# Weight and token rows that run on over group borders, with the input norm and the head issued in another order

## The chip, the cores and the metric

The kernel runs on one core of a Trainium2 chip. A core has five engines with a queue each: TensorE (PE in the profile, with its weight loads as PEld), VectorE (DVE), ScalarE (ACT), GpSimd (POOL) and SyncE (SP), which here only starts transfers. Transfers from the device's memory are started on the queues of SP, ACT and POOL. The metric is the device time of one execution in microseconds; lower is better.

## The reference

One step of a decoder layer for 256 prompt tokens and 8 sample tokens, all in float32, model width 2048. All weight products of the layer run over the 264 tokens together.

```python
def layer(x, conv_buf, h0, C0, n0, m0, mk, mv, ...):
    xn = rmsnorm(x, g_mix)
    z = xn @ w_in                                  # 2048 -> 5128
    xr, conv_new = causal_conv(z[..., OFF_RGX:OFF_RGG], conv_buf, conv_w, conv_b)
    r = jax.nn.sigmoid(block_diag(xr, w_rg_a, b_rg_a))
    ig = jax.nn.sigmoid(block_diag(xr, w_rg_x, b_rg_x))
    h_rg, h_last = rglru(xr, r, ig, rg_lambda, h0)  # uses softplus(-rg_lambda)
    y_rg = rmsnorm((h_rg * jax.nn.gelu(z[..., OFF_RGG:OFF_Q])), g_rg_out)
    ...
    h_ml, C_new, n_new, m_new = mlstm(q, k, v, logi, logf, C0, n0, m0)
    h_ml = rmsnorm(h_ml, g_ml_out.reshape(ML_HEADS, ML_DV)).reshape(B, L, ML_WIDTH)
    y_ml = h_ml * jax.nn.sigmoid(z[..., OFF_O:OFF_I])
    x = x + jnp.concatenate([y_rg, y_ml], axis=-1) @ w_out
    xq = (rmsnorm(x, g_xa) @ w_xa_q).reshape(B, L, XA_HEADS, XA_DH)
    ...                                            # attention over 256 memory tokens
    x = x + o @ w_xa_o
    xf = rmsnorm(x, g_ffn)
    x = x + (jax.nn.silu(xf @ w_ffn_gate) * (xf @ w_ffn_up)) @ w_ffn_down   # 2048 -> 5632 -> 2048
```

The memory's keys and values (`mem @ w_xa_k`, `mem @ w_xa_v`, after a norm) and a last norm of x come on top; the states and the keys and values are outputs too.

## The kernel before

**Tiles.** Activations stand transposed: 128 features on the partitions, 264 tokens along them. A feature chunk c of 128 is one row of 264 words, and four chunks share a tile of the pool `B` (26 tiles of `SLOT` = 1088 words); the norms' and products' operands are `HL` pairs, one tile for the high and one for the low part. A weight block (2048 inputs by 128 outputs) comes in two halves into `raw` (5 tiles) by SP's queue. `split_half` writes its high part on ACT (a copy rounded to fp32r) and its low part on DVE (the difference) into a tile `W` (4 tiles): per chunk a row of 264 words, 128 high, 128 low and 8 unused. So each row, of weights and of tokens, starts 1,056 bytes behind the one before it, which is 32 bytes more than four times 256. A half has 8 rows in two groups of four; the second group starts `SLOT` words behind the first, 32 words (128 bytes) further than the rows would have run on. The tile of the next four token chunks starts at a slot of its own in the same way. Both borders fall together, after every fourth chunk.

**Steps.** The list `steps` holds one step for each weight block. A step runs 16 chunks, each with the three matmuls of `mm3` (weights high with tokens high, high with low, low with high; the weights are the stationary operand, 264 token columns stream), so 48 matmuls into one of four PSUM banks `mm`. `evac` functions read the bank one step later. Steps 0 to 3 are special (`pe_first`): each takes four chunks of the tokens for all four first outputs, so that work can begin before all of x is there; their four banks (two `ax`, two `mm`) are read out after step 3. Then come the rest of `w_in`, `w_out`, the attention's q, k, v, o and, from about half of the time on, the feed-forward blocks.

**Side work.** Recurrences, gates, norms and attention are Python generators (`rg_gen`, `ml_gates`, `ml_norm`, `mem_gen` and others) that `pump` advances between the issue of two steps, by priced clocks of DVE and ACT. Small products in them write banks `ax`: `token_sums` sums a row of squares over the partitions (one output column for each 128 tokens, in plain fp32, which the profile shows as two matmuls each), and `spread` lays the resulting column out along the tokens again.

**Order.** Only SP's order is that of the code. On the other engines a scheduler orders the instructions by a simulated time line and by priorities, so the place in the code isn't the place on the engine.

**Head.** x (`xres`) and the first weights come on SP's queue in the order x 0-1, weights, x 2-3, weights and so on; the small vectors `vecs` on ACT's queue in two pieces. `warm(7)` runs seven matmuls on ones before there is data. The input norm adds up squares of 16 chunks with 16 ACT operations and 15 DVE additions into `acc_x` during steps 1 to 4 (`sumsq`); its token sums, the reciprocal root on DVE (`rsqrt`, tiles `c`) and the spread are `norm_x`, issued after step 4; ACT then writes `rstd`, which the evacuations of the first outputs need. `rg_coef` (with `log1p`) makes a coefficient out of `rg_lambda` by 20 small DVE operations on tiles `t` of 8 columns, and one on ACT.

In the profile most instructions carry line 63, that of the helper `Engine`; tiles tell them apart.

Of the kernel before, what the change touches and what calls it, by code (L numbers as in the profile page):

```python
# [10 lines left out]
F32 = mybir.dt.float32  # L11
# [6 lines left out]
P = 128  # L18
# [6 lines left out]
H = 4  # L25
# [58 lines left out]
def layer_kernel(ctx: ExitStack, tc, xT, memT, vec, wrg, w_in, w_out, w_q, w_k, w_v, w_o,  # L84
# [26 lines left out]
    def B(shape, dt=F32, skip=0):  # L111
        return view(sb.tile([P, SLOT], dt, tag="B", bufs=NB, name=nm("B")), shape, skip)
# [8 lines left out]
    class Arr:  # L121


        def __init__(self, nb, w=N, dt=F32):
            self.t, self.nb, self.w, self.dt = {}, nb, w, dt

        def tile(self, q):
            if q not in self.t:
                self.t[q] = B([P, min(4, self.nb), self.w], self.dt)
            return self.t[q]  # L130

        def __call__(self, c):
# [1 line left out]

    class HL:
        def __init__(self, nb, w=N):
            self.h, self.l = Arr(nb, w, F32R), Arr(nb, w, F32R)

        def __call__(self, c):
            return self.h(c), self.l(c)  # L140
# [1 line left out]
    class Side:  # L142
# [5 lines left out]
        def both(self, c):  # L148
            q, j = divmod(c, 2)
            if q not in self.t:  # L150
                self.t[q] = B([P, 2, 2 * T + 8], F32R, skip=16 * (q % 2))
            return self.t[q][:, j, : 2 * T]

        def __call__(self, c):
# [28 lines left out]
    def split_half(i, h, parts=1):  # L183
        if i >= len(steps):
            return
        cols = steps[i][1]
        lo, hi = h * 1024, min(cols, (h + 1) * 1024)
        w = sb.tile([P, 2, SLOT], F32R, tag="W", bufs=4, name=nm("W"))
        ng = (hi - lo) // 512
        rows = w[:, 0:ng, LEAD: LEAD + 4 * ROW].rearrange("p g (r x) -> p g r x", x=ROW)  # L190
        raw = raws[i, h][:, : hi - lo].rearrange("p (g r x) -> p g r x", r=4, x=P)
        pieces = [(slice(0, ng), slice(0, 4))]
        if parts > 1:
            pieces = [(slice(g, g + 1), slice(r, r + 8 // parts)) for g in range(ng) for r in range(0, 4, 8 // parts)]
        fused = i == GATES
        with tc.high_priority():
            for g, r in pieces:
                src, wh = raw[:, g, r, :], rows[:, g, r, 0:P]
                low = rows[:, g, r, P: 2 * P]
                if fused:  # L200
                    wh, low, src = wh[:, :, :, 0:64], wh[:, :, :, 64:P], src[:, :, :, 0:64]
                st["split"] = act.activation(wh, src, AF.Copy)
                dve.tensor_sub(low, src, wh)
        splits[i, h] = w

    class W:
# [1 line left out]
            self.i = i  # L208

        def __call__(self, c):  # L210
            w, g, o = splits[self.i, c // 8], c % 8 // 4, LEAD + c % 4 * ROW
            return w[:, g, o: o + P], w[:, g, o + P: o + 2 * P]

        def wide(self, c):
            w = splits[self.i, c // 2][:, c % 2, LEAD: LEAD + 4 * ROW].rearrange("p (r x) -> p r x", x=ROW)
            return w[:, :, 0:P], w[:, :, P: 2 * P]

    def mm3(ps, a, b, start, stop):
# [42 lines left out]
    def finish(cond):  # L261

        for _ in range(10000):
            if cond():
                return
            pump(1e12)
        raise RuntimeError("side work does not end")

    def bank(tag="mm"):
        return psm.tile([P, 512], F32, tag=tag, bufs=4, name=nm(tag))  # L270
# [294 lines left out]
    def ml_gates():  # L565
        R = ml["R"]
        li, u, e, lf, b, g, M = (R(j)[0:4] for j in range(7))
        yield STEP
        dve.scalar_tensor_tensor(e, u, -1.0, u, op0=OP.mult, op1=OP.min)
        act.activation(e, e, AF.Exp)  # L570
        yield 0.4
        log1p(lf, e)
        yield 6.0
        dve.tensor_scalar(u, u, 0.0, None, op0=OP.min)
        dve.tensor_sub(lf, u, lf)

# [24 lines left out]
        i4 = ident[0:4, 0:4]  # L601
        for j in range(2):
            pe.transpose(ps[:, 64 + 4 * j: 68 + 4 * j], g[:, j * P: j * P + P], i4)
        for j, w0 in enumerate(WIN):
            pe.transpose(ps[:, 72 + 4 * j: 76 + 4 * j], b[:, w0: w0 + P], i4)
# [185 lines left out]
    def ml_norm():  # L791

        while not (ml["pg"].done and ml["sg"].done):
            yield STEP
        hh = hT["t"]
        a = B([P, H, N])
        for h in range(H):
            for vb in range(2):
                act.activation(hh(2 * h + vb)[:, T:N], nums[:, 2 * h + vb, :], AF.Copy)
            sumsq(a[:, h, :], hh(2 * h), True)  # L800
            sumsq(a[:, h, :], hh(2 * h + 1), False)
            yield 0.35
        yield STEP
        ps = bank("ax")
        for h in range(H):
# [460 lines left out]
    with tc.high_priority():  # L1266
        for c in range(KC):
            split(*xn(c), xres[:, c, :], V("g_mix", c))
            if c == 1:
                split_half(0, 0, 4)  # L1270
            elif c == 3:
                split_half(0, 1, 2)

    pend = []
    for i, (src, cols, pef, evf, need) in enumerate(steps):
# [145 lines left out]
```

## Time and profile before

| | us |
|---|---|
| median of 3 runs (lowest to highest) | 1566.51 (1564.78 to 1567.93) |
| the profiled execution | 1565.63 |
| its span | 1563.9 |
| mean granted clock of TensorE | 0.995 |
| PE busy | 1545.7 |
| DVE busy | 1057.5 |
| ACT busy | 786.2 |

PE is busy for 99% of the span, but its matmuls overlap, so a busy PE can still be slower or faster: what tells is how far apart the matmuls start. The chain of work groups stretches in which PE goes from matmul to matmul with nothing else between; a stretch's length over its count is the pace of one matmul. Waits are read from the idle time before an instruction, the granted clock from tables by time window.

### The profile page before, as it was taken

Reading aid. Unit: us, or ns where it says so; the run is one execution under the profiler, and the core shown is the slowest. Engines: PE = TensorE matmul, PEld = TensorE weight load, DVE = VectorE, ACT = ScalarE, POOL = GpSimd, SP = SyncE. Lnnn points to the kernel's source line nnn. Section 1 sums busy time; section 2 is a strip of 40 time slices with the busy share of each in tenths; the row PEclk is TensorE's granted clock in tenths of the full one; section 3 lists DMA queues with packets and bytes.
Section 4 is the critical chain, followed back from the end, with each engine's and each line's share of the span. In section 5 each row is a group of like instructions: output and inputs, shape, how many; then the busy total and the mean of one; then the engine's idle time right before and its main releaser. Section 6 shows DMA issues by size and latency. Waiting matters only on the chain.

```text
span 1563.9 us, 30136 instructions
## 1 busy us (share of the span) xinstructions
PE 1545.7 (99%) x12084; PEld 1511.2 (97%) x12084; DVE 1057.5 (68%) x2024; ACT 786.2 (50%) x1249; POOL 124.5 (8%) x190
## 2 busy tenths in 40 slices
PE   9999999999999999999999999999999999999997
PEld 9999999999999888899999999999999999999997
DVE  7976987787699989876655555545555545555554
ACT  7475765664455656555444444334444433444463
POOL 0001210000134333310000000000000000000000
PEclk9999999999999999999999999999999999999999
DMA  8546984547689887855555555555555555555563
GB/s 292 177 162 209 296 285 170 190 148 254 251 299 346 324 297 250 319 169 186 176 176 187 177 186 180 186 179 186 178 188 176 188 179 186 179 186 179 159 183 103
DMA packets 92172, 326.01 MB, mean 208 GB/s; under 512 B 10784, under 2 KB 11216, under 8 KB 92032
## 3 DMA queue, kind: packets, MB, share of 16 engines
q1 hardware_dynamic: 76608, 270.70, 51.8%
q0 software_dynamic: 15136, 53.16, 9.7%
q8 instruction: 94, 1.54, 0.4%
q14 instruction: 46, 0.38, 0.1%
q10 hardware_dynamic: 288, 0.23, 0.1%
HBM read 312.78 MB, written 11.28 MB: 207 GB/s over the span
## 4 chain that ended last, share of the span: by engine, by line
PE 96%; DVE 2%; ACT 1%; DMA 0%; issue 0%; SPq 0%; DVEq 0%; ACTq 0%
PE mm L63 91%; PE ax L63 5%; DVE B L63 1%; ACT B L63 1%; DVE W L63 0%; DMA xres<-xT 0%; ACT W L63 0%; ACT L63 0%; DVE xres L63 0%; DVE c L63 0%; ACT t L63 0%; SPq L1260 0%; ACT rstd L63 0%; SPq L1254 0%; DVE acc_x L63 0%
## 5 line engine op out<-in xcount | busy, mean ns | idle before, releaser
L63 PE MATMUL mm<-B,W 128*128 128x264 f32 (+2 forms) x11008 | 1378.3, 286 | 4.3 <-DVE B L63 2.2
L63 PEld LDWEIGHTS mm<-B,W 128*128 128x128 f32 x11008 | 1354.8, 188 | 16.3 <-DVE W L63 2.5
L63 ACT ACTIVATE W<-raw 128x1024 fp32r<-128x1024 f32 (+2 forms) x518 | 536.5, 1037 | 667.4 <-PE mm L63 460.6
L63 DVE TENSOR_TENSOR W<-raw,W 128x1024 fp32r<-128x1024 f32 (+2 forms) x518 | 621.3, 1201 | 366.0 <-ACT W L63 364.9
L63 PE MATMUL mm<-W,B 128*128 128x512 f32 x384 | 92.0, 394 | 0.0
L63 PEld LDWEIGHTS mm<-W,B 128*128 128x128 f32 x384 | 71.0, 188 | 15.3
L63 DVE TENSOR_TENSOR t<-mm,rstd 128x264 f32<-128x264 f32 x104 | 44.9, 432 | 47.1 <-PE mm L63 46.6
L1313 POOL TENSOR_TENSOR B<-B,rstd 128x264 f32<-128x264 f32 x4 | 2.8, 739 | 861.6 <-ACT rstd L63 861.6
L63 DVE TENSOR_TENSOR xres<-xres,mm 128x264 f32<-128x264 f32 x80 | 34.2, 428 | 40.5 <-PE mm L63 40.5
L63 DVE SCALAR_TENSOR_TENSOR B<-B,dw 128x256 f32<-128x256 f32 x128 | 55.6, 489 | 4.0 <-ACT dw L63 4.0
L63 DVE SCALAR_TENSOR_TENSOR dw<-B,qsm,dw 128x256 f32<-128x256 f32 x96 | 49.7, 526 | 0.4
L63 PE MATMUL ax<-B,B 128*128 128x256 f32 (+3 forms) x288 | 48.3, 308 | 0.0
L63 PEld LDWEIGHTS ax<-B,B 128*128 128x128 f32 x288 | 40.7, 190 | 3.1 <-DVE B L63 0.7
L1005 POOL TENSOR_TENSOR dr<-dw,dr 128x256 fp32r<-128x256 f32 x32 | 35.0, 1097 | 106.8 <-ACT dr L63 105.6
L63 ACT ACTIVATE B<-xres,vecs 128x264 fp32r<-128x264 f32 (+1 forms) x64 | 31.1, 503 | 3.6 <-DMA xres<-xT 1.4
L63 ACT ACTIVATE t<-xres 128x264 f32<-128x264 f32 x60 | 23.7, 413 | 15.3 <-DVE xres L63 15.3
L994 POOL DMA_DIRECT2D B<-kcT x32 | 17.3, 542 | 142.7 <-DVE B L63 133.7
L63 ACT ACTIVATE B<-t 128x264 fp32r<-128x264 f32 (+1 forms) x60 | 24.2, 409 | 4.0 <-DVE t L63 3.8
L63 DVE TENSOR_TENSOR acc_x<-acc_x,t 128x264 f32<-128x264 f32 x59 | 25.3, 428 | 1.1 <-ACT t L63 0.5
L63 DVE SCALAR_TENSOR_TENSOR B<-xres,vecs,B 128x264 fp32r<-128x264 f32 x48 | 22.7, 488 | 4.2 <-ACT B L63 4.2
L63 ACT ACTIVATE t<-t 128x264 f32<-128x264 f32 (+1 forms) x61 | 24.8, 406 | 1.3 <-DVE t L63 1.2
L63 ACT ACTIVATE dw<-B,qsm 128x256 f32<-128x256 f32 x32 | 16.2, 508 | 17.0 <-DVE B L63 10.2
(151 smaller groups left out, 652.6 us busy)
## 6 DMA issues: line engine op xcount, KB each, us to landing
raw<-w_gu SPq DMA_DIRECT2D x176, 512.0 KB, 3.6
raw<-w_in SPq DMA_DIRECT2D x80, 512.0 KB, 4.6
raw<-w_d SPq DMA_DIRECT2D x80, 512.0 KB, 3.6
raw<-w_out SPq DMA_DIRECT2D x32, 512.0 KB, 4.1
B<-kcT POOLq DMA_DIRECT2D x32, 512.0 KB, 8.3
raw<-w_q SPq DMA_DIRECT2D x32, 512.0 KB, 4.2
B<-vcT POOLq DMA_DIRECT2D x32, 512.0 KB, 8.8
raw<-w_k SPq DMA_DIRECT2D x32, 512.0 KB, 7.1
```

The lines of the kernel that those rows point to most:

```text
L63: return f(*a, **k)
L994: pool_e.dma_start(kc, kcT[h, b])
L1005: pool_e.tensor_sub(wr[:, 1], acc, wr[:, 0].bitcast(F32))
L1313: e.tensor_mul(st["y"](c), st["y"](c), r)
```

## The change

**Rows.** The tile `W` becomes one run: the eight rows of a half follow each other by 264 words without the 32-word jump. Every second token tile of an `HL` starts 32 words later (`lead`), so the rows of a tile run on where those of the tile before stopped, as starts modulo 256 bytes. `Side` tiles get four starts in turn rather than two.

**Head.** 12 rather than 7 warm matmuls; the first quarter of the first weights moves from SP's queue to ACT's, between the two pieces of `vecs`. Nothing in the code moves `rg_coef`, but the scheduler now places its small operations into the head.

**Input norm.** The squares are four ACT operations of four chunks each, three DVE additions of 1,056 columns and one `tensor_reduce`, issued in steps 1 to 3; the rest of the norm is `first_norm`.

**Small sums.** `later` puts small PE products into a list and `drip`, called after each chunk's three matmuls, issues one of them; the generator waits in steps until its list is empty. The products of `ml_gates`, `ml_norm` and the input norm go this way. This sets the order of the code; the scheduler still has the last word.

```diff
@@ tiles
-                self.t[q] = B([P, min(4, self.nb), self.w], self.dt)
+                self.t[q] = B([P, min(4, self.nb), self.w], self.dt, skip=self.lead * (q % 2))
...
-            self.h, self.l = Arr(nb, w, F32R), Arr(nb, w, F32R)
+            self.h, self.l = Arr(nb, w, F32R, 32), Arr(nb, w, F32R, 32)
...
-                self.t[q] = B([P, 2, 2 * T + 8], F32R, skip=16 * (q % 2))
+                self.t[q] = B([P, 2, 2 * T + 8], F32R, skip=16 * (q % 4))
@@ split_half
-        w = sb.tile([P, 2, SLOT], F32R, tag="W", bufs=4, name=nm("W"))
-        ng = (hi - lo) // 512
-        rows = w[:, 0:ng, LEAD: LEAD + 4 * ROW].rearrange("p g (r x) -> p g r x", x=ROW)
-        raw = raws[i, h][:, : hi - lo].rearrange("p (g r x) -> p g r x", r=4, x=P)
...
+        w = sb.tile([P, 2 * SLOT], F32R, tag="W", bufs=4, name=nm("W"))
+        nr = (hi - lo) // P
+        rows = w[:, LEAD: LEAD + nr * ROW].rearrange("p (r x) -> p r x", x=ROW)
+        raw = raws[i, h][:, : hi - lo].rearrange("p (r x) -> p r x", x=P)
+        pieces = [slice(r, r + nr // parts) for r in range(0, nr, nr // parts)]
@@ class W
-            w, g, o = splits[self.i, c // 8], c % 8 // 4, LEAD + c % 4 * ROW
-            return w[:, g, o: o + P], w[:, g, o + P: o + 2 * P]
+            w, o = splits[self.i, c // 8], LEAD + c % 8 * ROW
+            return w[:, o: o + P], w[:, o + P: o + 2 * P]
@@ side work
+    def later(*fs, after=0):
+        k = [after, list(fs)]
+        drips.append(k)
+        return k
+
+    def drip(all=False):
+        while drips and (all or drips[0][0] <= 0):
+            k = drips[0]
+            k[1].pop(0)()
+            if not k[1]:
+                drips.pop(0)
+            if not all:
+                return
+        if drips:
+            drips[0][0] -= 1
@@ head
-    warm(7)
+    warm(12)
...
     act.dma_start(vecs[:, 0:16], vec[:, 0:16])
+    act.dma_start(raw_half(0, 0)[:, 0:512], w_in[0][:, 0:512])
     act.dma_start(vecs[:, 16:], vec[:, 16:])
@@ ml_norm (ml_gates alike)
-        for h in range(H):
-            token_sums(ps, a[:, h, :], 3 * h)
-
+        k = later(*[lambda h=h: token_sums(ps, a[:, h, :], 3 * h) for h in range(H)])
+        while k[1]:
+            yield STEP
@@ proj
                 mm3(ps[:, :n], w(c), rhs(c), c == 0, c == nch - 1)
+                drip()
@@ loads of the head
-        r = raws[0, h // 2] if h % 2 else raw_half(0, h // 2)
-        sp.dma_start(r[:, h % 2 * 512: h % 2 * 512 + 512], w_in[0][:, h * 512: h * 512 + 512])
+        if h:
+            r = raw_half(0, 1) if h == 2 else raws[0, h // 2]
+            sp.dma_start(r[:, h % 2 * 512: h % 2 * 512 + 512], w_in[0][:, h * 512: h * 512 + 512])
@@ input norm
+    def square(q):
+        s = B([P, 4, N])
+        act.activation(s, xres[:, 4 * q: 4 * q + 4, :], AF.Square)
+        if q == 0:
+            sq["t"] = s
+            return
+        dve.tensor_add(sq["t"], sq["t"], s)
+        if q == 3:
+            dve.tensor_reduce(acc_x, sq["t"].rearrange("p c n -> p n c"), axis=AX.X, op=OP.add)
+
+    def first_norm():
+        ps = bank("ax")
+        k = later(lambda: token_sums(ps, acc_x, N), after=2)
+        while k[1]:
+            yield STEP
+        v, r = ctile(3), ctile(3)
+        dve.tensor_scalar(v, ps[:, N: N + 3], 1.0 / D, EPS, op0=OP.mult, op1=OP.add)
+        rsqrt(v, r)
+        yield STEP
+        spread(ps, [r[:, j: j + 1] for j in range(3)])
+        act.activation(rstd, ps[:, :N], AF.Copy)
+        yield 0.1
...
-        if 1 <= i < 5:
+        if 1 <= i < 4:
             with tc.issue_after(st["split"].ins):
-                for c in range(4 * i - 4, 4 * i):
-                    sumsq(acc_x, xres[:, c, :], c == 0)
-        if i == 4:
-            fn = side(norm_x(), -1)
+                for q in ((0, 1), (2,), (3,))[i - 1]:
+                    square(q)
+        if i == 3:
+            fn = side(first_norm(), -1)
```

**What this moves on the engines.** First DVE in the head, from the split of the first tokens on (`B` of `xres` and `vecs` is the low part of tokens, `W` of `raw` the low part of weights, `t` are the small operations of `rg_coef`). Before:

```order
L63 SCALAR_TENSOR_TENSOR B_133<-xres,vecs,B_132 128x264 x2
L63 TENSOR_TENSOR W_138<-raw_114,W_138 128x2x128 x2
L63 SCALAR_TENSOR_TENSOR B_133<-xres,vecs,B_132 128x264 x2
L63 TENSOR_TENSOR W_138<-raw_114,W_138 128x2x128 x2
L63 TENSOR_TENSOR W_151<-raw_118,W_151 128x4x128 x2
L63 SCALAR_TENSOR_TENSOR B_157<-xres,vecs,B_156 128x264 x4
```

After:

```order
L63 TENSOR_TENSOR W_143<-raw_96,W_143 128x2x128 x2
L63 SCALAR_TENSOR_TENSOR B_138<-xres,vecs,B_137 128x264
L63 SCALAR_TENSOR_TENSOR t_607<-vecs 128x8
L63 SCALAR_TENSOR_TENSOR B_138<-xres,vecs,B_137 128x264
L63 TENSOR_SCALAR t_613<-t_609 128x8
L63 RECIPROCAL t_613<-t_613 128x8
L63 TENSOR_TENSOR W_143<-raw_96,W_143 128x2x128
L63 TENSOR_TENSOR t_612<-t_609,t_613 128x8
L63 TENSOR_TENSOR W_143<-raw_96,W_143 128x2x128
L63 TENSOR_TENSOR t_617<-t_612 128x8
L63 TENSOR_TENSOR W_156<-raw_123,W_156 128x4x128
L63 TENSOR_SCALAR t_613<-t_617 128x8
```

The small operations on `t`, which ran during steps 4 and 5 before, now stand between the first token and weight splits; fourteen more of them follow behind these rows, most between the four parts of the next token split and the weight splits behind it.

Next PE at the end of the norm's first part (`ax` of `ones` and `acc_x` is the token sums, x3 for three windows of tokens). Before, inside step 5, with `W_452` and `W_455` its two weight halves:

```order
L63 MATMUL mm_579<-B_157,W_452 128x264
L63 MATMUL mm_579<-B_156,W_452 128x264 x2
L63 MATMUL mm_579<-B_157,W_452 128x264
L63 MATMUL ax_523<-ones,acc_x 128x1 x3
L63 MATMUL mm_579<-B_156,W_452 128x264
L63 MATMUL mm_579<-B_166,W_455 128x264
L63 MATMUL mm_579<-B_167,W_455 128x264
```

After, where the row with `W_376` behind the sums is the last matmul of step 4 and `W_436` belongs to step 5:

```order
L63 MATMUL mm_442<-B_182,W_376 128x264
L63 MATMUL mm_442<-B_181,W_376 128x264 x2
L63 MATMUL mm_442<-B_182,W_376 128x264
L63 MATMUL ax_435<-ones,acc_x 128x1 x3
L63 MATMUL mm_442<-B_181,W_376 128x264
L63 MATMUL mm_549<-B_137,W_436 128x264
L63 MATMUL mm_549<-B_138,W_436 128x264
```

The sums moved from the middle of step 5 to a place ahead of the last matmul of step 4. The spread that follows them stands between the last matmul of step 5 and the first of step 6, as before.

Last PE at the sums of `ml_norm`, before in the step that ends with `W_2851`:

```order
L63 MATMUL mm_2955<-B_176,W_2851 128x264 x2
L63 MATMUL mm_2955<-B_177,W_2851 128x264
L63 MATMUL ax_2907<-ones,B_2750 128x1 x12
L63 MATMUL mm_2955<-B_176,W_2851 128x264 x2
L63 MATMUL mm_2955<-B_177,W_2851 128x264
L63 MATMUL mm_2955<-B_176,W_2851 128x264
L63 MATMUL mm_3045<-B_132,W_2949 128x264
```

After:

```order
L63 MATMUL mm_3057<-B_181,W_2954 128x264 x2
L63 MATMUL mm_3057<-B_182,W_2954 128x264
L63 MATMUL ax_2943<-ones,B_2852 128x1 x12
L63 MATMUL mm_3057<-B_181,W_2954 128x264
L63 MATMUL mm_3148<-B_137,W_3051 128x264
L63 MATMUL mm_3148<-B_138,W_3051 128x264
L63 MATMUL mm_3148<-B_137,W_3051 128x264 x2
```

The twelve sums are still in one piece; they stand two steps later and one matmul ahead of the end of the step.

More of the change, by code (lines that the diff above doesn't have):

```diff
@@ L121, in layer_kernel, with __init__ @@
     class Arr:
-        def __init__(self, nb, w=N, dt=F32):
-            self.t, self.nb, self.w, self.dt = {}, nb, w, dt
+        def __init__(self, nb, w=N, dt=F32, lead=0):
+            self.t, self.nb, self.w, self.dt, self.lead = {}, nb, w, dt, lead
         def tile(self, q):
             if q not in self.t:
-                self.t[q] = B([P, min(4, self.nb), self.w], self.dt)
+                self.t[q] = B([P, min(4, self.nb), self.w], self.dt, skip=self.lead * (q % 2))
             return self.t[q]
@@ L187, in split_half @@
         lo, hi = h * 1024, min(cols, (h + 1) * 1024)
-        w = sb.tile([P, 2, SLOT], F32R, tag="W", bufs=4, name=nm("W"))
-        ng = (hi - lo) // 512
-        rows = w[:, 0:ng, LEAD: LEAD + 4 * ROW].rearrange("p g (r x) -> p g r x", x=ROW)
-        raw = raws[i, h][:, : hi - lo].rearrange("p (g r x) -> p g r x", r=4, x=P)
-        pieces = [(slice(0, ng), slice(0, 4))]
-        if parts > 1:
-            pieces = [(slice(g, g + 1), slice(r, r + 8 // parts)) for g in range(ng) for r in range(0, 4, 8 // parts)]
+        w = sb.tile([P, 2 * SLOT], F32R, tag="W", bufs=4, name=nm("W"))
[3 more added lines that the diff above has]
+        pieces = [slice(r, r + nr // parts) for r in range(0, nr, nr // parts)]
         fused = i == GATES
         with tc.high_priority():
-            for g, r in pieces:
-                src, wh = raw[:, g, r, :], rows[:, g, r, 0:P]
-                low = rows[:, g, r, P: 2 * P]
+            for r in pieces:
+                src, wh, low = raw[:, r, :], rows[:, r, 0:P], rows[:, r, P: 2 * P]
                 if fused:
-                    wh, low, src = wh[:, :, :, 0:64], wh[:, :, :, 64:P], src[:, :, :, 0:64]
+                    wh, low, src = wh[:, :, 0:64], wh[:, :, 64:P], src[:, :, 0:64]
                 st["split"] = act.activation(wh, src, AF.Copy)
@@ L210, in __call__ @@
         def __call__(self, c):
-            w, g, o = splits[self.i, c // 8], c % 8 // 4, LEAD + c % 4 * ROW
-            return w[:, g, o: o + P], w[:, g, o + P: o + 2 * P]
+            w, o = splits[self.i, c // 8], LEAD + c % 8 * ROW
+            return w[:, o: o + P], w[:, o + P: o + 2 * P]
         def wide(self, c):
-            w = splits[self.i, c // 2][:, c % 2, LEAD: LEAD + 4 * ROW].rearrange("p (r x) -> p r x", x=ROW)
+            o = LEAD + c % 2 * 4 * ROW
+            w = splits[self.i, c // 2][:, o: o + 4 * ROW].rearrange("p (r x) -> p r x", x=ROW)
             return w[:, :, 0:P], w[:, :, P: 2 * P]
@@ L265, in finish @@
                 return
+            drip(True)
             pump(1e12)
         raise RuntimeError("side work does not end")
+    drips = []
+    def later(*fs, after=0):
[12 more added lines that the diff above has]
+            drips[0][0] -= 1
     def bank(tag="mm"):
@@ L597, in ml_gates, with scal, turn @@
         ps = bank("ax")
-        for h in range(H):
+        i4 = ident[0:4, 0:4]
+        def scal(h):
             pe.matmul(ps[:, h * 16: h * 16 + 16], ident[0:4, h: h + 1].to_broadcast([4, P]), x16,
                       start=True, stop=True)
[L601 to L605, printed above, removed]
+        def turn(o, src):
+            pe.transpose(ps[:, o: o + 4], src, i4)
+        k = later(*[lambda h=h: scal(h) for h in range(H)],
+                  *[lambda j=j: turn(64 + 4 * j, g[:, j * P: j * P + P]) for j in range(2)],
+                  *[lambda j=j, w0=w0: turn(72 + 4 * j, b[:, w0: w0 + P]) for j, w0 in enumerate(WIN)])
+        while k[1]:
+            yield STEP
         act.activation(bcs, ps[:, 0:64].rearrange("p (h j) -> p h j", j=16), AF.Copy)
@@ L804, in ml_norm @@
         ps = bank("ax")
-        for h in range(H):
-            token_sums(ps, a[:, h, :], 3 * h)
+        k = later(*[lambda h=h: token_sums(ps, a[:, h, :], 3 * h) for h in range(H)])
+        while k[1]:
+            yield STEP
         r, v, f = ctile(12), ctile(12), ctile(12)
@@ L1272, in layer_kernel @@
                 split_half(0, 1, 2)
+    sq = {}
+    def square(q):
[10 more added lines that the diff above has]
+        k = later(lambda: token_sums(ps, acc_x, N), after=2)
+        while k[1]:
+            yield STEP
+        v, r = ctile(3), ctile(3)
+        dve.tensor_scalar(v, ps[:, N: N + 3], 1.0 / D, EPS, op0=OP.mult, op1=OP.add)
+        rsqrt(v, r)
+        yield STEP
+        spread(ps, [r[:, j: j + 1] for j in range(3)])
+        act.activation(rstd, ps[:, :N], AF.Copy)
+        yield 0.1
     pend = []
```

## Prediction

> **What bounds the kernel now.** I read the page first (busy times, the chain's shares, the matmul group), then PE's waits, then the chain in order of time.
>
> ```profile
> PE 1545.7 (99%) x12084; PEld 1511.2 (97%) x12084; DVE 1057.5 (68%) x2024; ACT 786.2 (50%) x1249; POOL 124.5 (8%) x190
> PE 96%; DVE 2%; ACT 1%; DMA 0%; issue 0%; SPq 0%; DVEq 0%; ACTq 0%
> L63 PE MATMUL mm<-B,W 128*128 128x264 f32 (+2 forms) x11008 | 1378.3, 286 | 4.3 <-DVE B L63 2.2
> PE mm L63 <- DVE B L63: 2.2, 1, 2.2
> PE mm L63 <- DVE W L63: 2.0, 2, 1.4
> PE ax L63 <- ACT W L63: 1.7, 1, 1.7
> ```
>
> The first three rows say that PE carries the time. The last three are all of its long waits for other engines (total us, times, longest): some 6 us, 0.4% of the time. Anything larger has to change how fast matmuls follow each other. That pace isn't one number. Five stretches of the chain (start, length, what):
>
> ```profile
> 201.52 28.82 PE mm L63 x236
> 264.40 59.96 PE mm L63 x494
> 351.52 40.62 PE mm L63 x332
> ...
> 703.34 86.86 PE mm L63 x714
> 797.83 751.42 PE mm L63 x6232
> ```
>
> The same instruction, 264 columns on 128 rows, takes 122.1, 121.4, 122.3, 121.7 and 120.57 ns (length over count). The last stretch is nearly all of the feed-forward, 48% of the time, and keeps the fast pace for 751 us. The second thing that moves the pace is the granted clock. Windows of 3.41 us, with PE's matmuls (x) and the clock (PEclk):
>
> ```profile
> 4.28:7.69 3.41, 1.65 (x8) 1.02 (x7) 1.95 (x5) 2.25 (x7) 0.00 (x0) 1.00 0.97 334
> 7.69:11.10 3.41, 3.27 (x15) 3.15 (x15) 2.92 (x7) 2.74 (x8) 0.00 (x0) 0.50 1.04 423
> 11.10:14.52 3.42, 3.42 (x30) 3.42 (x29) 2.98 (x6) 3.15 (x6) 0.00 (x0) 1.00 1.02 398
> 48.65:52.07 3.42, 3.42 (x18) 3.42 (x17) 3.42 (x11) 0.39 (x3) 0.00 (x0) 0.50 0.30 104
> 233.00:236.40 3.40, 3.40 (x17) 3.40 (x17) 2.82 (x10) 1.68 (x3) 0.00 (x0) 0.50 1.02 416
> ```
>
> A window at half clock gets 15 to 18 matmuls through rather than 30: 12 to 15 matmuls of 0.1206 us, so 1.45 to 1.8 us each. There are three. The first follows a window with 1.65 us of PE work, the second the stall below, the third a run of tiny sums (24 at 230.18).
>
> **Head.** Rows of PE, DVE and the chain there:
>
> ```profile
> 1.12 3.32 PE L63 MATMUL mm<-ones 128*128 128x128 f32 x14 [1.12 <-DVE ones L63]
> 6.11 5.06 PE L63 MATMUL ax<-B,W 128*128 128x264 f32 x20 [1.67 <-ACT W L63]
> 10.72 1.72 DVE L63 SCALAR_TENSOR_TENSOR B<-xres,vecs,B 128x264 fp32r<-128x264 f32 x4 [0.49 <-ACT B L63]
> 12.88 2.36 DVE L63 TENSOR_TENSOR W<-raw,W 128x1024 fp32r<-128x1024 f32 x2 [0.45 <-ACT W L63]
> 15.56 2.46 PE ax L63 x20
> 40.22 0.76 DVE L63 SCALAR_TENSOR_TENSOR t<-t,t 128x8 f32<-128x8 f32 x4
> ```
>
> Twelve warm matmuls are 24 on the array. The 14 run until 4.44 at about 0.22 us each; ten more at 0.11 us (half of that, the clock granted after 4.28 being full) end at 5.5. The window from 4.28 then holds 1.65 + 1.1 = 2.7 us of work instead of 1.65, and I take it that no half-clock window follows: up to 1.8 us. But PE can't use all of it. At 15.56 it needs the high and low halves of the next weights; the low part of their first half is done at about 14.06 (two splits from 12.88, 1.18 each), so today 1.5 us early. The change puts 20 small operations of `rg_coef` at 0.19 us (0.76 over 4) on DVE ahead of or among these splits: 3.8 us less the 0.9 us that DVE waits (0.49 and 0.45) and less what waits earlier absorb. Seven of them, 1.3 us, sit among the four token splits right ahead of that weight split, so 1.3 - 0.45 = 0.9 us of delay: done at 14.9 rather than 14.06, a gain of 15.56 - 14.9 = 0.7 us, and I take -0.8 with the earlier second token pair. Bounds: -1.8 (all of the window) and +0.8 (window stays, or DVE is 0.8 us past 15.56). The first weights leave from ACT's queue, issued at the time at which `vecs`'s second piece left, so I leave PE's first real matmul at 6.1.
>
> **Input norm.** Around the stall:
>
> ```profile
> 44.51 1.06 ACT L63 ACTIVATE W<-raw 128x1024 fp32r<-128x1024 f32 x1 [1.84 <-PE mm L63]
> 45.15 0.81 PE L63 MATMUL ax<-ident,c 128*128 128x128 f32 x6 [0.73 <-DVE c L63]
> 45.60 1.23 DVE L63 TENSOR_TENSOR W<-raw,W 128x1024 fp32r<-128x1024 f32 x1 [0.60 <-ACT W L63]
> 45.99 0.39 ACT L63 ACTIVATE rstd<-ax 128x264 f32<-128x264 f32 x1 [0.43 <-PE ax L63]
> 46.74 0.90 DVE L63 TENSOR_TENSOR B<-ax,rstd 128x256 f32<-128x256 f32 x4
> 48.19 1.06 PE L63 MATMUL mm<-B,W 128*128 128x264 f32 x5 [2.24 <-DVE B L63]
> ```
>
> Sums one step earlier mean that the roots (`c`) are there when step 5 ends, and the spread runs at about 44.2 instead of 45.15. That wait isn't what ends last. The bank that step 6 needs is freed by the evacuation at 46.74, and it stands on DVE behind the split at 45.60, which waits for ACT's at 44.51, which waits for PE to release a `W` tile at the end of step 5. In the new order both splits still stand ahead, so PE still starts at 48.2: 0, bounds -1.4 (the evacuation follows `rstd` at once: spread 44.2 + 0.84 as from 45.15 to 45.99, + 0.75 to the evacuation = 45.8 rather than 46.74, and the clock window half saved) and +0.6. The additions (15 of 0.43 before; three and a reduction of about 1.25 now, by the 1024-column split's 1.23) and squares lie in DVE's and ACT's waits for PE.
>
> **Sums of the gates and of `ml_norm`.** They are not spread in the new order; the twelve stay together, and their 24 tiny matmuls cost what they cost. The half-clock window behind them may come or not, by where they fall among the windows: 0, bounds -1.6 and +1.6. Their successors move by a step or two, into waits that I price by PE's longest wait for a weight split (1.4 above): no more than that, and inside the same bound.
>
> **Rows.** W and tokens now step by 32 bytes modulo 256 without a jump. The instruction counts and shapes of PE, ACT and DVE splits are the same, so the only effect there can be is on PE's pace. Today's rows repeat their starts after every four chunks (12 matmuls), and the new ones after eight. That one stream holds 120.57 ns for 6232 matmuls and another 121.65 for 714 at the same starts says that there are at least two patterns that PE's stream locks into, and the rows alone don't choose. I expect that the fast one hangs on the jump that comes back after every twelfth matmul, since nothing else repeats in the feed-forward, and that without it the stream runs at the pace of the stretches that never held it. The nearest is the long one at 264.40: 121.37. So 6232 x (121.37 - 120.57) = +5.0 us, and the others of this shape stay as they are. How many those are, a row by shapes tells:
>
> ```profile
> L63 PE MATMUL mm<-B,W 128*128 128x264 f32 x10496 | 1285.8, 284 | 4.3 <-DVE B L63 2.2 <-DVE W L63 2.0
> ```
>
> 10496 - 6232 = 4264. Bounds: -4.0 (the jump is what costs: these 4264 come down from about 121.5 to 120.57, and the feed-forward stays) and +11.1 (all 6232 at 122.35, the pace at 351.52).
>
> **Sum.** 1565.63 - 0.8 + 0 + 0 + 5.0 = 1569.8 for an execution like the profiled one; that lies 0.9 below the median of the runs, half a half-clock window, so 1570.5 for the median, +0.25%. About 0.2% is what a measurement of this kernel can tell from no change: 1563.4 to 1569.6.
>
> **Rivals.**
> First, rows don't matter to PE. For it: both paces occur today with the same layout. Then only the head counts: 1566.5 - 0.8 = 1565.7, no change. The Trainium skill ("SBUF — State Buffer", section "SBUF: two separate sides") says just this: PE, ACT and DVE's own ports never wait on anyone, so no start of a row should cost. By that page alone the sum would be 1565.7. The two paces of one instruction above fit it badly, unless they have a cause besides SBUF; no row here tells.
> Second, on the other side: the jump is what breaks the stream, and the stretches at 121.4 to 122.3 come down. Time 1566.5 - 4.0 - 0.8 = 1561.7, faster; it decides as soon as 3 us of the 4 come. Against it: the fastest pace is held with a jump at every fourth chunk.
> Third, the windows decide. If the head stays at half clock and DVE's small operations make PE wait at 15.56 (+0.8), and one more window of half clock follows the sums (+1.6): 1568.9 with unchanged rows. The windows follow a fixed grid of 3.41 us, whose phase to the program nothing in the kernel sets. The Trainium skill ("TensorE: Matmul & The Clock Gate", section "What's actually happening") calls the window free-running, which the three starts here, multiples of 3.413 us apart, agree with.
>
> **Chances.** Slower pace 0.54 (1566 to 1576 by itself; of the 0.54, 0.43 slower by over 0.2%, 0.11 within); rows without effect 0.15 (within 0.09, faster 0.06); jump was the cost 0.26 (faster 0.23, within 0.03); windows 0.05 (within 0.04, slower 0.01). So faster 0.29, within 0.27, slower 0.44. The range from 1559 to 1576 holds the second rival with the full head gain (1560.7) and most of the way to the upper bound (1576.8).
>
> **What would show it.** In the feed-forward's stretch of the chain, the pace: 121.4 confirms the main term, 120.6 the first rival, and less elsewhere the second. In the head: clock 1.00 in all windows behind 4.3 and an `ax` x20 at 14.8 instead of 15.56. Around the stall: the spread with no wait for `c`, yet `mm` still waiting for DVE `B` for 4 us after step 5. I am wrong if PE's stream finds a pace that no stretch shows today; nothing in the profile excludes one below 120.57.

## The result and the profile after

The changed kernel took 1573.20 us (median of 6 runs, 1572.10 to 1576.03) where the kernel before took 1565.68 in the same session: a ratio of 1.0049, 95% interval 1.0036 to 1.0062. So it is slower by 7.5 us. Measured once more beside the last experiments it was 1572.35 against 1566.20, a ratio of 1.0043 (1.0029 to 1.0056). The time lies in the range that was forecast and on the side that was forecast. The reason is another one. One execution of a later experiment (the gates' products alone) took 6303.24 us at a granted clock of 0.231 and is left out of the figures given for it.

From the changed kernel, the page's busy times, and PE's waits (total us, times, longest us):

```profile
PE 1549.3 (99%) x12094; PEld 1513.8 (96%) x12094; DVE 1058.1 (67%) x2013; ACT 786.1 (50%) x1237; POOL 124.6 (8%) x190
PE mm L63 <- DVE t L63: 4.2, 2, 3.6
PE mm L63 <- DVE B L63: 3.1, 1, 3.1
PE mm L63 <- DVE W L63: 1.9, 2, 1.3
PE ax L63 <- DVE B L63: 0.9, 1, 0.9
```

The first wait is new: PE waits for a DVE instruction that writes `t`, twice, 4.2 us in all. Next the chain of waits of the changed kernel (start, length, what), with some of the stretches that were shown of before:

```profile
15.39 2.71 PE ax L63 x20
...
48.14 11.05 PE mm L63 x77
...
358.55 40.60 PE mm L63 x332
...
406.82 22.59 PE mm L63 x187
...
711.65 86.67 PE mm L63 x714
...
805.99 750.13 PE mm L63 x6232
```

Three things are read from it. First, where the time went: step 6 starts at 48.14 (48.19 before), the stretch of 332 matmuls at 358.55 (351.52), the feed-forward's stretch at 805.99 (797.83). So 7.0 of the 8.2 us that are lost by then were lost between 48 and 359; the new wait is 4.2 of them. Second, the feed-forward did not lose: 6232 matmuls took 750.13 us, 120.37 ns each, against 751.42 and 120.57 before. The row starts made it 1.3 us faster. Third, the middle of the program lost a little; for comparison a row of the kernel before that wasn't shown yet:

```profile
399.78 22.65 PE mm L63 x187
```

From this stretch of 187 to that of 714 it was 703.34 - 399.78 = 303.56 us before and is 711.65 - 406.82 = 304.83 now, 1.3 us more.

The place of the wait, from the time lines of PE and DVE in the changed kernel (start, busy, engine, operation, count, idle time before it and what ended it). `B<-B,bcs,t` and the `t<-B,B` behind it are the state update of one sample row; `t<-mm,rstd` is the evacuation of one block of the recurrence's gate, the product that frees a bank `mm`:

```profile
227.94 6.07 PE L63 MATMUL mm<-B,W 128*128 128x264 f32 x48 [0.58 <-DVE t L63]
237.58 5.66 PE L63 MATMUL mm<-B,W 128*128 128x264 f32 x32 [3.57 <-DVE t L63]
```

```profile
233.37 0.48 DVE L63 SCALAR_TENSOR_TENSOR B<-B,bcs,t 128x256 f32<-128x256 f32 x1
233.88 0.29 DVE L63 SCALAR_TENSOR_TENSOR t<-B,B 128x128 f32<-128x128 f32 x1
...
235.13 1.23 DVE L63 TENSOR_TENSOR W<-raw,W 128x1024 fp32r<-128x1024 f32 x1 [0.62 <-ACT W L63]
236.28 0.48 DVE L63 SCALAR_TENSOR_TENSOR B<-B,bcs,t 128x256 f32<-128x256 f32 x1
236.79 0.29 DVE L63 SCALAR_TENSOR_TENSOR t<-B,B 128x128 f32<-128x128 f32 x1
...
237.01 0.43 DVE L63 TENSOR_TENSOR t<-mm,rstd 128x264 f32<-128x264 f32 x1
```

PE stands from 234.0 to 237.58 without a free bank, while DVE has 0.6 us of idle time, a weight split and a sample row's update ahead of the evacuation that would free one. In the time line of the kernel before, the last sample row's update ends at 226, and evacuations of this kind follow at 228.3, 230.5 and 231.8.

A table by windows shows half-clock windows in the changed kernel too (PEclk is the third column from the right):

```profile
4.30:7.70 3.40, 3.40 (x20) 3.40 (x20) 2.10 (x5) 1.93 (x5) 0.00 (x0) 1.00 0.94 304
7.70:11.10 3.40, 2.48 (x19) 2.19 (x19) 2.71 (x11) 2.17 (x6) 0.00 (x0) 1.00 1.04 423
48.00:51.00 3.00, 2.86 (x13) 2.89 (x14) 3.00 (x11) 0.90 (x6) 0.00 (x0) 0.50 0.49 168
126.50:129.50 3.00, 3.00 (x15) 3.00 (x15) 3.00 (x5) 0.88 (x2) 0.00 (x0) 0.50 0.56 176
239.50:242.00 2.50, 2.50 (x14) 2.50 (x13) 2.36 (x11) 1.13 (x4) 0.00 (x0) 0.50 0.07 25
```

There are three again. The one in the head is gone, one behind the wait at 124 has come (116 matmuls from 126.29 on take 15.91 us, where they took 14.35 before), and the third now follows the new wait. Their number and places differ from one execution to the next.

### The profile page after: what moved, and what is told of

It reads as the page before. It is cut to its first block, busy times and chain, and to the rows that moved or that the text cites. A ratio compares the mean times of both kernels' runs of the same rounds, so it can differ in the third digit from the quotient of the medians.

```text
span 1570.4 us, 30129 instructions
## 1 busy us (share of the span) xinstructions
PE 1549.3 (99%) x12094; PEld 1513.8 (96%) x12094; DVE 1058.1 (67%) x2013; ACT 786.1 (50%) x1237; POOL 124.6 (8%) x190
## 4 chain that ended last, share of the span: by engine, by line
PE 95%; DVE 3%; ACT 1%; DMA 0%; issue 0%; ACTq 0%; DVEq 0%
PE mm L63 90%; PE ax L63 5%; DVE B L63 2%; DVE W L63 1%; ACT B L63 0%; DMA vecs<-vec 0%; ACT W L63 0%; ACT L63 0%; DVE t L63 0%; DVE xres L63 0%; DVE c L63 0%; ACT t L63 0%; ACTq L310 0%; ACT rstd L63 0%; DVE acc_x L63 0%
## 5 line engine op out<-in xcount | busy, mean ns | idle before, releaser
L63 ACT ACTIVATE t<-xres 128x264 f32<-128x264 f32 x45 | 18.7, 415 | 15.3 <-DVE xres L63 15.3
L63 ACT ACTIVATE t<-B,B 128x128 f32<-128x128 f32 x64 | 21.4, 390 | 5.1 <-DMA B<-scr 5.1
```

The lines of the kernel that those rows point to most:

```text
L63: return f(*a, **k)
```

## The experiments

The theory after this reading, called "bank" below: `ml_gates` now gives its nine products to `later`, which issues one behind each chunk of the next step, and itself waits for whole steps until they are out. So it ends later, and `ml_sample`, which waits for it, starts later. Its updates then fall into the steps of the recurrence's gates. Both take temporaries from the six `t` tiles, so the evacuations come late, and PE runs out of banks. The rival "rows" is the prediction's main term: the new row starts cost some 5 us.

**The gates' products alone.** The kernel before, with this edit alone:

```diff
-        for h in range(H):
-            pe.matmul(ps[:, h * 16: h * 16 + 16], ident[0:4, h: h + 1].to_broadcast([4, P]), x16,
-                      start=True, stop=True)
...
+        k = later(*[lambda h=h: scal(h) for h in range(H)],
+                  *[lambda j=j: turn(64 + 4 * j, g[:, j * P: j * P + P]) for j in range(2)],
+                  *[lambda j=j, w0=w0: turn(72 + 4 * j, b[:, w0: w0 + P]) for j, w0 in enumerate(WIN)])
+        while k[1]:
+            yield STEP
```

> The kernel before, with only the products of ml_gates going through `later` and `drip`. Theory bank (the gates end later, so the sample rows' work runs later, and the evacuations of the recurrence's gates, which share the six `t` tiles with it, come late and PE waits for a PSUM bank): about 4.2 us more than before, the waits of PE for `t` in the changed kernel (4.2 in two waits), so +3.5 to +5.5, and PE's waits show DVE `t` with 3 us or more. Theory rows (the new row starts are what costs): no change, within 1 us of before.

Measured 1570.73 (median of six) against 1566.73: +4.0 us by the medians and 4.2 by the ratio, 1.0027 (1.0015 to 1.0038). PE's waits in this run, and then a row of its time line:

```profile
PE mm L63 <- DVE t L63: 4.2, 2, 3.6
```

```profile
235.66 7.50 PE L63 MATMUL mm<-B,W 128*128 128x264 f32 x40 [3.57 <-DVE t L63]
```

The same two waits, the longer one to the hundredth, with all rows, the head and the norm as before. Bank is confirmed; rows doesn't explain this run.

**All but the gates' products.** The changed kernel with the same edit undone.

> The changed kernel, with the products of ml_gates issued at once as before. Theory bank: 4 us less than the changed kernel, so 2 to 4 us above before (1568 to 1570), and no wait of PE for DVE `t`. Theory rows: as the changed kernel, 7 us above before.

Measured 1568.30 against 1566.73: +1.6, ratio 1.0009 (1.0000 to 1.0017). PE no longer waits for DVE `t` (its longest waits are 3.1 for `B` at step 6 and 1.3 for `W`). So this one edit makes most of the loss: 4.2 us when added to the kernel before, and some 5 to 6 when taken from the changed one, by the ratios 1.0049 or 1.0043 less 1.0009.

**Temporaries of their own.** To tell whether the late sample work costs time as such or only by the order that it forces on the evacuations, the changed kernel gets one line:

```diff
     def evac_rgg(n):
         def f(ps):
-            z = tmp()
+            z = ltmp()
```

> The changed kernel, whose recurrence gate evacuation takes its temporary from the ring of three `lt` tiles rather than from the six `t` tiles that the sample work uses. Nothing else. Theory bank: the sample work is as late as in the changed kernel, but PE no longer waits for DVE `t`: 4 us less than the changed kernel, 1568 to 1570. Theory that the later sums themselves, or the work of the samples as such, cost the time: unchanged, 1573.

Measured 1569.20 against 1566.73, ratio 1.0012 (1.0003 to 1.0021). The sample work runs as late as in the changed kernel, but the gate's evacuations, now on `lt`, follow on DVE after a weight split and one operation of the samples. First the stretch of PE that held both waits, 359 matmuls without an idle time, then DVE:

```profile
203.07 45.02 PE L63 MATMUL mm<-B,W 128*128 128x264 f32 x359
```

```profile
231.38 1.23 DVE L63 TENSOR_TENSOR W<-raw,W 128x1024 fp32r<-128x1024 f32 x1 [0.48 <-ACT W L63]
232.53 0.48 DVE L63 SCALAR_TENSOR_TENSOR B<-B,bcs,t 128x256 f32<-128x256 f32 x1
233.29 0.43 DVE L63 TENSOR_TENSOR lt<-mm,rstd 128x264 f32<-128x264 f32 x1 [0.28 <-PE mm L63]
...
234.43 1.23 DVE L63 TENSOR_TENSOR W<-raw,W 128x1024 fp32r<-128x1024 f32 x1 [0.16 <-ACT W L63]
...
237.37 1.23 DVE L63 TENSOR_TENSOR W<-raw,W 128x1024 fp32r<-128x1024 f32 x1
...
239.27 0.43 DVE L63 TENSOR_TENSOR lt<-mm,rstd 128x264 f32<-128x264 f32 x1 [0.28 <-PE mm L63]
```

Now DVE waits for PE before these two evacuations, not the reverse. The late work by itself doesn't cost these 4 us; the ring of temporaries that it shares with the evacuations does. The 1.9 us above before that are left by the ratio are not explained by this run.

**The rows alone.** The kernel before with the new starts of `W`, `HL` and `Side` tiles, nothing else.

> The kernel before, with only the new starts of rows (W tiles, HL tiles, Side tiles). Theory rows: +5.0 us as predicted (bounds -4.0 and +11.1). Theory bank with the paces of the changed kernel's profile (feed-forward 120.37 ns instead of 120.57, 6232 times, so -1.3; about +1.2 in the attention; +0.3 in steps 8 to 16): within 1 us of before.

Measured 1567.82 against 1566.73, ratio 1.0005 (0.9996 to 1.0014): no change that can be told. Four stretches of its chain:

```profile
81.67 11.66 PE mm L63 x96
203.15 29.54 PE mm L63 x236
...
705.72 86.67 PE mm L63 x714
800.06 750.13 PE mm L63 x6232
```

The stretches with the same counts before took 28.82 (x236), 86.86 and 751.42, and 11.59 for the 96:

```profile
81.51 11.59 PE mm L63 x96
```

So new rows do move the pace, up in some steps (122.1 to 125.2 ns in the 236; 120.7 to 121.5 in the 96) and down in others (120.57 to 120.37 in the feed-forward), and the sum can't be told from nothing.

**Rows without the Side tiles.** The same without the line `skip=16 * (q % 4)`.

> The kernel before with the new row starts of the W and HL tiles only; the Side tiles keep their two starts in turn. With all new row starts (the run of rows only), the steps of the attention between 470 and 690 us took 1.1 us longer in the trace and the feed-forward 1.3 us less. If the four starts of Side make the attention's loss: 1.2 us less than with all new starts, so about 0.4 us below before. If the loss comes from the W and HL rows: as the run of rows only, about 0.8 us above before.

Measured 1568.36 against 1566.17, ratio 1.0015 (1.0006 to 1.0024), so slower by 2 us, where 0.4 less or 0.8 more was expected; the interval still overlaps that of the rows alone. From its chain:

```profile
406.76 22.59 PE mm L63 x187
...
711.38 86.67 PE mm L63 x714
805.72 750.13 PE mm L63 x6232
```

711.38 - 406.76 = 304.62 us: 1.1 of the 1.3 us of the middle stay when `Side` is as before, so the W and HL rows make them. The rest of its loss isn't settled: the profiled execution, the slowest of its eleven (1572.26), has three stretches of half clock that are two windows long, as in this row,

```profile
46.20:53.00 6.80, 5.83 (x26) 5.86 (x27) 6.80 (x23) 1.68 (x11) 0.00 (x0) 0.51 0.26 84
```

and whether the rows bring these about or chance does can't be told from one profile.

**The head alone.**

```diff
-    warm(7)
+    warm(12)
...
+    act.dma_start(raw_half(0, 0)[:, 0:512], w_in[0][:, 0:512])
...
+        if h:
+            r = raw_half(0, 1) if h == 2 else raws[0, h // 2]
```

> The kernel before with only the head changed: 12 warm matmuls, first weights from ACT's queue. The prediction's term: -0.8 (bounds -1.8 and +0.8). By the changed kernel's profile, where the second piece of vecs lands at 8.34 and DVE waits for it: -0.2, within 0.5 of before.

Measured 1564.76 against 1566.17, ratio 0.9993 (0.9984 to 1.0002): 1.4 us less by the medians, 1.1 by the ratio, not safely told from none. PE in its head by the time line, and then the second `ax` x20 by the chain:

```profile
1.12 5.49 PE L63 MATMUL mm<-ones 128*128 128x128 f32 x24 [1.12 <-DVE ones L63]
6.26 3.63 PE L63 MATMUL ax<-B,W 128*128 128x264 f32 x24
```

```profile
14.73 2.44 PE ax L63 x20
```

It starts at 14.73 rather than at 15.56 in the chain before. But two kernels with the old head, whose profiled executions have no half-clock window there (the gates' products alone and the rows without `Side`), start it as early, at 14.76 and 14.54; a row of the first:

```profile
14.76 2.43 PE ax L63 x20
```

So the gain is that of the missing window, and the moved weights show none of their own. The window is missing in all seven profiles with twelve warm matmuls, and in two of the six with seven. In this kernel the operations of `rg_coef` are still late; in the run of the norm alone they stand in the head, so it is the norm's edit that lets the scheduler put them there.

**The norm alone.** The kernel before with `square` and `first_norm`.

> The kernel before with only the input norm changed (four squares, three additions, a reduction, sums ahead of the last matmul of step 4). The prediction's term: 0 (bounds -1.4 and +0.6), PE starts step 6 four us after step 5's end, as before, since the evacuation stands behind the weight split. Rival: the reciprocal root was the late part, and step 6 starts 1 us earlier.

Measured 1566.11 against 1566.17, ratio 1.0000 (0.9991 to 1.0009). PE still waits 3.1 us for the evacuation at step 6 (2.2 before, with 0.7 for `c` ahead of it). The prediction's 0 holds, and the rival's 1 us doesn't.

**The stall at step 6, taken away.** The W and HL rows and the norm as changed, `evac_rgg` on `lt`, the rest as before, and three orders fixed:

```diff
-    first = [bank("ax"), bank("ax"), bank(), bank()]
+    first = [bank(), bank(), bank("ax"), bank("ax")]
...
             for c in range(nch):
+                if i == 5 and c == 11:
+                    cm = tc.issue_after(st["spread"].ins)
+                    cm.__enter__()
                 mm3(ps[:, :n], w(c), rhs(c), c == 0, c == nch - 1)
...
+            if i == 6:
+                with tc.issue_after(st["rstd1"].ins), tc.issue_after(st["ev", 3].ins):
+                    split_half(i + LS, 1)
```

Here `st["spread"]`, `st["rstd1"]` and `st["ev", 3]` are the last matmul of the spread, ACT's write of `rstd` and DVE's last evacuation of the four first outputs.

> W and HL rows as changed, the changed input norm, the gate evacuation on the lt tiles, Side, head and the sums of gates and ml_norm as before; and three orders fixed: the spread of the input norm after 33 of 48 matmuls of step 5 (its roots were there at 41.9 in the changed kernel, when step 5 still had 2 us to go), the first outputs' evacuation ahead of the second weight split of step 7, and the banks mm of the first outputs read out ahead of the banks ax. If the stall of 4 us at the end of step 5 is only the evacuation standing behind the split: 3 us or more less, and 1.6 more where no half-clock window follows, so 4 to 5.5 us below before (1561 to 1563). If something else holds step 6: about as before, within 1 us.

Measured 1566.04 against 1566.17, ratio 0.9998 (0.9989 to 1.0006). The stall itself went, as the time line of PE shows:

```profile
42.41 0.73 PE L63 MATMUL ax<-ident,c 128*128 128x128 f32 x6
42.99 7.28 PE L63 MATMUL mm<-B,W 128*128 128x264 f32 x58
```

PE runs on from step 5 into step 6 without a gap, where 4 us lay before. But the whole kernel didn't gain. From its chain:

```profile
77.01 11.97 PE mm L63 x96
```

These 96 matmuls, 11.59 before and 11.66 with the new rows, took 11.97, a pace of 124.7 ns. They start 4.5 us earlier than before (77.01 against 81.51); at the stretch of 332 the kernel is 1.5 us later than before (353.00 against 351.52). The profile has four windows of half clock, three before, and how the loss divides between them and the rows isn't settled.

**The same with the old rows.** All rows as before, the changed head and norm, and the three orders.

> All rows as before (W, HL, Side), the sums of the gates and of ml_norm as before, the changed head and input norm, and the three orders of the run with the spread in step 5. In that run steps 6 to 8 took 5.5 us less than before, but steps 9 to 16 ran at 124.7 ns a matmul, and half-clock windows took more. If that loss belongs to the new rows: 5 us and the head's 1 us below before, about 1560. If PE's stream falls into the slow pace whenever no half-clock window comes before it, with old rows too: 1563 to 1565.

Measured 1563.23 against 1566.20, ratio 0.9983 (0.9974 to 0.9992): 3 us less. By the total that is what the theory of the slow pace expected; by the pace it isn't, for that is the one of before:

```profile
76.23 11.59 PE mm L63 x96
```

So the slow pace in these steps belonged to the new rows. They start at 76.23 instead of 81.51, 5.3 us earlier, head and stall together. Only 3 us are left at the end; the rest went where PE waits for the weight splits behind the recurrence (a row of the time line, then two of a table by windows):

```profile
122.29 8.94 PE L63 MATMUL mm<-B,W 128*128 128x264 f32 x49 [1.59 <-DVE W L63]
```

```profile
121.60:125.02 3.42, 2.73 (x12) 2.73 (x13) 3.42 (x6) 1.77 (x5) 0.00 (x0) 0.50 0.44 135
125.02:128.44 3.42, 3.42 (x18) 3.42 (x17) 3.42 (x10) 0.90 (x1) 0.00 (x0) 0.50 0.72 192
```

PE comes there 5.3 us earlier, but DVE's split that it waits for only 3.9 (121.04 against 124.90), and two windows of half clock lie around the wait.

**New rows in the feed-forward alone.** The kernel of the last run, with the W rows of the feed-forward's steps and the HL tiles that they read in the new starts:

```diff
-                st[key] = HL(KC)
+                st[key] = HL(KC, lead=32 if key == "ffn" else 0)
...
+            if self.i >= ff[0]:
+                w, o = splits[self.i, c // 8], LEAD + c % 8 * ROW
+                return w[:, o: o + P], w[:, o + P: o + 2 * P]
```

> The run before this, with the new row starts of W and HL tiles in the feed-forward's steps alone, where the trace of the changed kernel has 120.37 ns instead of 120.57. If the fast pace belongs to the rows of these steps: 1.3 us less than the run before this. If it depends on how the stream comes in from the steps ahead: no gain, or a loss.

Measured 1561.90 against 1566.20, ratio 0.9975 (0.9963 to 0.9986), the fastest of all and faster than both kernels. Against the run before this the 1.3 us are as expected, but the two intervals overlap; the pace tells it. Its last stretch:

```profile
795.33 750.13 PE mm L63 x6232
```

The pace of 120.37 is there although everything ahead has the old rows. So it belongs to these steps' own rows.

**The changed kernel again**, beside the last two.

> The changed kernel once more, beside the two others on one chip. Theory bank plus rows plus head from their own runs (4.6 + 0.8 - 1.1): 4.3 us above before; by the first measurement: 7.5 above. The difference is what half-clock windows and the combination add.

Measured 1572.35 against 1566.20, +6.2. The parts by themselves (by the ratios 4.2 for the gates' products, 0.8 for the rows, -1.1 for the head, 0 for the norm) add up to 3.9, and about 2 us of the combination, 3.6 by the first measurement, are not explained by them. The run of all but the gates' products has such a rest too: 1.4 by its ratio, where its parts give -0.3. The sums of `ml_norm` were not run alone. In that run they are changed, in the run of the rows alone they are not, and from the stretch of 236 to that of 332 both take the same time (350.94 - 201.48 = 149.46 and 352.60 - 203.15 = 149.45 us), so no cost of theirs shows there. The intervals of the single ratios are some 0.1%, 1.5 us, wide on either side, and the half-clock windows fall differently: the profiles have between one and six.

## Why the prediction was right in time and wrong in reason

- **Rows, +5.0.** This is the step that failed: "I expect that the fast one hangs on the jump that comes back after every twelfth matmul, since nothing else repeats in the feed-forward". Without the jump the feed-forward ran at 120.37 ns, faster than in the kernel before, and the rows alone made 0.8 to 1.1 us, not told from none. That the forecast was slower by some 4 us and the kernel came out slower by 7.5 is luck: the loss came from a term that was put at 0. The trace before held no row with other starts in the same steps, so nothing in it could carry that step. The prediction named such an outcome ("a pace that no stretch shows today") and gave it no chance of its own. Its paces were also read too high: a short stretch's length holds more than its matmuls, and from the start of one matmul to that of the next the trace before has 121.2 at 264.40 and 121.6 at 351.52, not 121.4 and 122.35, so by its own rule the term was +3.7 and its upper bound +6.2. (In the sum, 1569.8 + 0.9 is 1570.7, not 1570.5.)
- **Rows don't matter (first rival).** By the total it is nearest: 1.0005. As a mechanism it isn't so: the paces of three stretches changed with the rows, in both directions. Between the kernel before and the rows alone nothing that runs differs but starts of rows, and 6232 matmuls take 751.42 and 750.13 us. The sentence of the Trainium skill used with it ("SBUF — State Buffer", section "SBUF: two separate sides"), that PE never waits on anyone there, is about contention for the ports; that no start of a row should cost was the prediction's own conclusion, and these paces are against it.
- **Sums of the gates, 0 with 1.6 either way.** The sign of the result sits here. The step read: "Their successors move by a step or two, into waits that I price by PE's longest wait for a weight split (1.4 above): no more than that". This step failed as well. The successors were the sample rows' updates, and what they met was not a weight split but the evacuation of PE's banks: 4.2 us of waits, and 4.2 by the ratio measured alone. The prediction followed the moved products on PE's queue and not the generator that waits behind them, nor the tiles that its work shares with the evacuations.
- **Head, -0.8.** Alone -1.1 (ratio 0.9993, up to 1.0002). In the changed kernel the row moved from 15.56 to 15.39 only (15.22 in the second measurement's profile, 14.99 and 14.67 in the two other kernels with all of its head), since the second piece of `vecs` landed late and DVE's first operation on `t` stood waiting ahead of the token split, as the chain of the changed kernel shows:

```profile
1.73 6.61 DMA vecs<-vec
8.36 0.17 DVE t L63
8.52 0.40 DVE B L63
```

  The piece landed at 1.73 + 6.61 = 8.34. The prediction followed the weights to ACT's queue and did not count the piece of `vecs` behind them; in this profile that was the term's miss, 0.6 us. The gone half-clock window (7.70 to 11.10 at 1.00) was as forecast, though two profiles with the old head lack it too. The 24 warm matmuls last until 6.6 by their row in the run of the head alone (1.12 + 5.49, the same in the changed kernel) and not 5.5: the ten more took 0.22 us each like the first fourteen, at a granted clock of 1.00 from 0.9 on, so the halving to 0.11 was a misreading.
- **Norm, 0.** Right, alone 1.0000, for the reason given: the evacuation stands behind the split. The last experiments show that the stall, with the half-clock window behind it, was worth some 5 us in its place.
- **Windows.** Three of half clock before, three after, in other places. As a rival by themselves they did not decide; behind the new wait and the one at 124 they add to the loss.

## What to carry to other kernels

When a generator or helper is made to wait, follow what starts after it, engine by engine, until it meets something that frees a resource PE needs; the price of the wait is that meeting, not the few products that were moved. A ring of temporaries shared by background work and by evacuations can make the background work part of the critical path; here one ring of its own for the evacuation took most of the loss back with a single line. A layout that moves the pace of a stream should be measured stage by stage and kept where it helps: the same rows were worth -1.3 us in the feed-forward and cost more than that elsewhere (1.3 in the middle, 0.7 in the stretch of 236).

## What the runs showed of the hardware

The pace of one and the same matmul (264 columns, weights of 128 by 128, full clock) took several values by row starts and stage. From the start of one matmul to that of the next the traces have 120.35 and 120.56 ns in the feed-forward (new and old rows), 120.7 in the 96 with old rows, 121.4 or 124.7 there with new ones, 121.65 and 124.7 in the 236 (old and new). Length over count, used above, gives up to 0.8 ns more on short stretches. The pace is steady within a stage for thousands of matmuls and the same to a hundredth of a microsecond in several runs (750.13 in eight profiles, all those with the new rows there), so it is a property of the stream and not noise. In the steps of the 96 matmuls the same new rows gave 121.4 in five profiles, which all have a half-clock window around 48 to 53, right ahead of these steps, and 124.7 in the two that have none there (the run with temporaries of their own and the one without the stall); with the old rows the pace stayed at 120.7 in either case. Another stretch has two paces with the same old rows: the 332 run at 120.7 in three profiles and at 121.5 to 121.6 in three others. So the starts of rows don't set the pace alone, and how the stream is entered seems to matter too; that is argued from these few runs, and what it hangs on stays open.
